# A hybrid decoder trunk: the mixer's 24 modulation tiles on GpSimd, ScalarE and VectorE instead of TensorE

## The chip, the cores and the metric

The kernel runs on one core of a Trainium2 chip. The core has a matrix engine (PE, TensorE), a vector engine (DVE, VectorE), a scalar engine (ACT, ScalarE), a general engine (POOL, GpSimd), and a queue (SP, SyncE) that issues most of the DMA transfers. Each engine works through its own instructions in order; semaphores order them against each other. PE writes its results into eight PSUM banks; everything else lies in SBUF. The metric is the device time of one execution in microseconds; a profiled execution gives, beside its time, a trace of every instruction.

## What is computed

Two layers over 256 positions of width 1024. Each layer has a mixer and a gated feed-forward, and each of these is wrapped in a modulation that a conditioning vector `c` sets:

```python
cs = jax.nn.silu(c)
mod = cs @ mod_w[layer] + mod_b[layer]          # 1024 -> 6 * 1024
sh1, sc1, g1, sh2, sc2, g2 = jnp.split(mod, 6, axis=-1)
h = rms_norm(x, norm_g[layer, 0]) * (1 + sc1) + sh1
x = x + g1 * mixer(h)       # layer 0: S5 state space + attention; layer 1: conformer convolution
h = rms_norm(x, norm_g[layer, 1]) * (1 + sc2) + sh2
x = x + g2 * conv_ffn(h)
```

The mixer of layer 0 projects `h` to a state-space part (32 groups of 16 channels with 64 complex states each) and to q, k, v of 8 heads. Their outputs are joined and projected. The change is about three of the twelve vectors of 1024: `g1`, `sc2` and `sh2` of layer 0, numbered 2, 4 and 3 in the code. They are matrix-vector products, each with a 1024 x 1024 block of `mod_w[0]`, that is 8 tiles of 128 x 1024 (512 KB each), 24 tiles in all. They are needed only after the mixer: the gate in `residual`, the scale and shift in `norm_gain` and `shift_cols`.

## The kernel before

All weights come as chunks of 128 x 1024 float32 in one order, `chunk_order`. `pump` issues the loads on SP in that order, each into the next free raw buffer: ten at the start (RAW_BUFS), four more, called ABT, when `s5_drive` has been placed. Most matmuls take float32 as a high and a low part: `split` has ACT copy a raw tile to `whi` and DVE subtract it to `wlo`, and three matmuls (high x high, high x low, low x high) make one product. `done` gives a raw buffer back and issues the next load.

The order of instructions on each engine is not the order of the text. `Plan` records every operation, estimates its cost and its dependences, and `arrange` places the operations of a stage by rank, which is the longest path behind an operation plus a hand-set or searched number per group (`BONUS`). The whole of `mixer0`, from the first load to the `glu` product, is one stage of this kind; the rest is placed in further stages. The matmuls of a bundle are placed as one.

The mixer stage computes, in this order of need: the layer's first modulation and the projection to u and q (`phase_a`); the poles, powers and tables of the state space (`s5_poles` to `s5_rot`, DVE and GpSimd, in the tile `arena` and the tile `CS`); k and v projections (`proj_k`, `proj_v`); the driven states (`s5_drive` on PE, `s5_state` on DVE: products with cosine and sine, four scans, and products again, the last of which writes Z); the outputs `s5_y` (PE, from KD, CA and Z); and attention by pairs of heads (`attn_score`, `attn_exp`, `attn_norm`, `attn_turn`, `attn_out`). Behind it `proj_o` multiplies the joined output with the abo chunks.

The three modulation vectors are made on PE between these. `mod_pe` takes each raw tile as the moving operand (512 columns at a time) and a 32-column version of `silu(c)`, `csv`, as the stationary one; four tiles go to four row groups of two banks, `B[6:8]`, which are the banks that `attn_turn` also uses. All 24 tiles add up in these two banks. Then `mod_evac` copies them to `mrow`, and `mod_sel` turns the rows into columns with eight small matmuls and adds the bias:

```python
nc.tensor.matmul(banks[half][g:g + 32, :], self.csv[:, j, f, :],
                 self.raw[("mp", l, s, f)][:, half * 512:half * 512 + 512], ...)
```

In the feed-forward of layer 0 other modulation tiles are already made on DVE, by `mod_dve`: one multiply of the raw tile by `cb` (silu(c) on every partition) with a running sum into one column of `modv`, and after eight of them the bias:

```python
self.nc.vector.scalar_tensor_tensor(self.junk, self.raw[c], 1.0, self.cb, op0=OP.mult, op1=OP.mult, accum_out=col)
```

Of the kernel before, what the change touches and what calls it, by code (L numbers as in the profile page):

```python
# [24 lines left out]
RAW_BUFS = 10  # L25
# [10 lines left out]
MD_STEP = (2, 1)  # L36
LN_MODS = [(1, 3), (1, 4)]
# [51 lines left out]
def chunk_order():  # L89
# [7 lines left out]
    def mp(l, s):  # L97
        return [("mp", l, s, f) for f in range(8)]

    a, b, c = mp(0, 2), mp(0, 4), mp(0, 3)  # L100
    order += [("k", 0), ("k", 1)] + a[:4] + [("k", 2), ("k", 3)] + a[4:]
    order += [("v", 0), ("v", 1)] + b[:4] + [("v", 2), ("v", 3)] + b[4:] + c
    order += [("abo", 4), ("abo", 5), ("glu", 0), ("glu", 1)]
    order += [("abo", i) for i in (6, 7, 0, 1, 2, 3)]
    md = [("md", l, s, f) for l, s in MD for f in range(8)]
    for i, c in enumerate(ffn_seq(0) + [("down", 0, i) for i in range(22)]):
        order.append(c)
        if md and i >= MD_FROM and (i % MD_STEP[0] < MD_STEP[1] if i < 44 else (i - 44) % MD_DOWN[0] < MD_DOWN[1]):
# [1972 lines left out]
```

## Time and profile before

| | us |
|---|---|
| median of 3 runs | 650.72 (647.98 to 651.05) |
| the profiled execution's time | 652.09 |
| its span, first to last instruction | 650.3 |

Nearly all instructions carry one line number, that of the planner's last line (L487), so they are told apart by the tiles that they write and read: `bank<-raw,csv` is a matmul of `mod_pe`, `wlo<-raw,whi` a low half, `junk<-raw,cb` a multiply of `mod_dve`. A matmul of float32 operands stands as two records. PEld is the weight load that goes with each matmul and overlaps it; its busy time is measured, while the end of a matmul is modelled. Times are from the span's start.

### The profile page before, as it was taken

The page shows a single profiled execution, that of the slowest core. Times are in us where ns is not written, and L with a number is a line of the kernel's source. Part 1 is how long each engine was busy: PE and PEld are TensorE (multiplying, and loading weights), DVE is VectorE, ACT ScalarE, POOL GpSimd, SP SyncE. Part 2 cuts the span into 40 slices and gives each one's busy share as a digit, 9 for nine tenths or more (in the row PEclk, how much of TensorE's full clock was granted, in tenths as well). Part 3 has the DMA queues.
Part 4 walks back from the last instruction along what each step waited for, and adds up shares of the span by engine and source line. Part 5 has one row for each costly group of instructions (what it writes and reads, how often), then busy time and mean ns, then how long its engine had stood idle before and what let it go on. Part 6 is the DMA issues. An engine that isn't in the chain of part 4 may idle for free.

```text
span 650.3 us, 13240 instructions
## 1 busy us (share of the span) xinstructions
PE 640.4 (98%) x5128; PEld 562.5 (87%) x5128; DVE 538.8 (83%) x1059; ACT 404.9 (62%) x736; POOL 41.2 (6%) x99
## 2 busy tenths in 40 slices
PE   8999999999999999999999999999999999999995
PEld 5789876899999999998899987568988888888885
DVE  8698996389999999999657999559999998997641
ACT  3479528897966666654446843377687766675431
POOL 4830000000000000000000222000000000000000
PEclk9999999999999999999999999999999999999998
DMA  8996888765489999999662798496476668764001
GB/s 325 405 377 224 291 324 300 316 217 210 134 288 320 325 331 303 338 328 365 195 196 81 245 325 245 154 380 263 135 280 199 201 214 259 217 210 164 1 0 66
DMA packets 45702, 158.50 MB, mean 244 GB/s; under 512 B 5535, under 2 KB 7112, under 8 KB 45640
## 3 DMA queue, kind: packets, MB, share of 16 engines
q1 hardware_dynamic: 43912, 153.84, 67.6%
q0 software_dynamic: 1152, 3.49, 1.9%
q8 instruction: 40, 0.66, 0.4%
q10 hardware_dynamic: 576, 0.33, 0.2%
q14 instruction: 22, 0.18, 0.1%
HBM read 153.10 MB, written 1.06 MB: 237 GB/s over the span
## 4 chain that ended last, share of the span: by engine, by line
PE 88%; DVE 7%; ACT 2%; DMA 1%; issue 1%; DVEq 0%; SPq 0%
PE bank L487 88%; DVE arena L487 4%; DVE wlo L487 1%; DMA raw<-w_in 1%; ACT CA L487 1%; DVE CS L487 1%; DVE U L487 1%; ACT whi L487 0%; ACT ABT L487 0%; DVE gp L487 0%; DVE nm L487 0%; DVE junk L487 0%; DVE h L487 0%; DVEq L2044 0%; DVE nt L487 0%
## 5 line engine op out<-in xcount | busy, mean ns | idle before, releaser
L487 PE MATMUL bank<-h,whi 128*128 128x256 f32 (+2 forms) x960 | 202.3, 303 | 0.2
L487 PEld LDWEIGHTS bank<-h,whi 128*128 128x128 f32 x960 | 152.4, 189 | 8.7 <-issue 1.0
L487 PE MATMUL bank<-h,wlo 128*128 128x256 f32 (+1 forms) x560 | 155.5, 283 | 0.0
L487 PE MATMUL bank<-h,whim 128*128 128x256 f32 (+1 forms) x664 | 149.1, 311 | 0.0
L487 PE MATMUL bank<-h,wlom 128*128 128x256 f32 x416 | 116.4, 281 | 0.0
L487 PEld LDWEIGHTS bank<-h,whim 128*128 128x128 f32 x664 | 108.2, 189 | 7.7
L487 PEld LDWEIGHTS bank<-h,wlo 128*128 128x128 f32 x560 | 104.5, 189 | 1.3 <-DVE CS L487 0.8
L487 DVE TENSOR_TENSOR wlo<-raw,whi 128x1024 fp32r<-128x1024 f32 x69 | 84.1, 1222 | 13.6 <-ACT whi L487 10.4
L487 ACT ACTIVATE whi<-raw 128x1024 fp32r<-128x1024 f32 x69 | 72.5, 1055 | 20.7 <-PE bank L487 13.7
L487 DVE TENSOR_TENSOR wlom<-raw,whim 128x1024 fp32r<-128x1024 f32 x60 | 72.9, 1222 | 10.5 <-ACT whim L487 10.3
L487 PEld LDWEIGHTS bank<-h,wlom 128*128 128x128 f32 x416 | 78.3, 188 | 0.1
L487 ACT ACTIVATE whim<-raw 128x1024 fp32r<-128x1024 f32 x60 | 62.6, 1054 | 22.7 <-PE bank L487 15.8
L487 PE MATMUL bank<-hv,whim 128*128 128x512 f32 (+1 forms) x236 | 67.7, 351 | 0.0
L487 PE MATMUL bank<-hv,whi 128*128 128x512 f32 x160 | 56.3, 393 | 0.0
L487 PE MATMUL bank<-hv,wlom 128*128 128x256 f32 x192 | 53.9, 281 | 0.0
L487 PEld LDWEIGHTS bank<-hv,whim 128*128 128x128 f32 x236 | 41.3, 189 | 6.2
L487 PE MATMUL bank<-hv,wlo 128*128 128x256 f32 x160 | 44.7, 279 | 0.0
L487 DVE SCALAR_TENSOR_TENSOR ac<-g,pp,ac 128x256 f32<-128x256 f32 x88 | 42.2, 482 | 2.5 <-ACT ac L487 0.8
L487 DVE SCALAR_TENSOR_TENSOR x<-bank,modv,x 128x256 f32<-128x256 f32 x54 | 25.6, 481 | 19.7 <-PE bank L487 19.1
L487 ACT ACTIVATE whi<-ABT 128x1024 fp32r<-128x1024 f32 x28 | 29.3, 1054 | 16.3 <-PE bank L487 15.3
L487 ACT ACTIVATE g<-bank 128x256 f32<-128x256 f32 x40 | 15.3, 382 | 36.4 <-PE bank L487 36.3
L487 PEld LDWEIGHTS bank<-hv,wlom 128*128 128x128 f32 x192 | 36.4, 190 | 0.0
(220 smaller groups left out, 1071.6 us busy)
## 6 DMA issues: line engine op xcount, KB each, us to landing
raw<-w_in SPq DMA_DIRECT2D x213, 512.0 KB, 5.3
ABT<-w_in SPq DMA_DIRECT2D x71, 512.0 KB, 4.9
a<-ap POOLq DMA_DIRECT2D x24, 142.0 KB, 5.4
x<-x_in SPq DMA_DIRECT2D x4, 256.0 KB, 4.2
arena<-scr SPq DMA_DIRECT2D x1, 1024.0 KB, 6.0
cb<-c_in SPq DMA_DIRECT2D x2, 512.0 KB, 4.9
kT<-bc_in SPq DMA_DIRECT2D x1, 512.0 KB, 11.4
out<-junk SPq DMA_DIRECT2D x2, 256.0 KB, 2.0
```

What stands on the lines that cost most here:

```text
L487: getattr(getattr(self.nc, eng), fn)(*a, **k)
```

## The change

The loads: the 24 chunks are packed the other way round, with 128 outputs on the partitions and the 1024 inputs along the row (`md` in place of `mp`), and they lie singly to threes between the chunks of k, v, abo and glu. The arithmetic: `mod_next` takes them one by one at written places of the mixer. Of three tiles, two are multiplied by `cb` on GpSimd in place and then copied by ACT with a running sum (`mod_pool`), and the third is one multiply with a running sum on DVE. `mod_bias` adds the bias to the columns at the end. `broadcast` makes `cb` for the mixer at the start: DVE multiplies the identity by silu(c), two matmuls with ones spread it over the partitions, ACT copies it out. `mod_pe`, `mod_evac` and `mod_sel` leave the mixer; `mod_pe` stays in the conformer. RAW_BUFS falls from 10 to 9, which makes room for the new tile. The planner's DMA rate goes from 370e3 to 390e3, and all numbers of BONUS are replaced, those of the loads too. ON_POOL leaves the later tiles on DVE, as they were.

```diff
-RAW_BUFS = 10
+RAW_BUFS = 9
...
+MIX_MOD = (1, 1, 0)
+ON_POOL = (0,)
...
-BONUS = {...}
+BONUS = {...}
...
-    a, b, c = mp(0, 2), mp(0, 4), mp(0, 3)
-    order += [("k", 0), ("k", 1)] + a[:4] + [("k", 2), ("k", 3)] + a[4:]
-    order += [("v", 0), ("v", 1)] + b[:4] + [("v", 2), ("v", 3)] + b[4:] + c
-    order += [("abo", 4), ("abo", 5), ("glu", 0), ("glu", 1)]
+    md = [("md", 0, s, f) for s in (2, 4, 3) for f in range(8)]
+    for c, n in zip([("k", 0), ("k", 1), ("k", 2), ("k", 3), ("v", 0), ("v", 1), ("v", 2), ("v", 3),
+                     ("abo", 4), ("abo", 5), ("glu", 0), ("glu", 1)], (1, 1, 1, 1, 2, 2, 2, 2, 3, 3, 3, 3)):
+        order += [c] + md[:n]
+        del md[:n]
...
-            return max(1.0 if op[4] == "rel" else 0.06, b / 370e3)
+            return max(1.0 if op[4] == "rel" else 0.06, b / 390e3)
...
+    def mod_pool(self, c):
+        _, l, s, f = c
+        w = self.raw[c]
+        self.nc.gpsimd.tensor_tensor(w, w, self.cb, op=OP.mult)
+        self.nc.scalar.activation(w, w, AF.Copy, accum_out=self.modv[l][:, s * 8 + f:s * 8 + f + 1])
+        self.done(c)
+
+    def mod_next(self, n):
+        for _ in range(n):
+            i = self.i_next
+            self.nc.group = "mod%d" % i
+            c = ("md", 0, (2, 4, 3)[i // 8], i % 8)
+            if MIX_MOD[i % len(MIX_MOD)]:
+                self.mod_pool(c)
+            else:
+                w = self.raw[c]
+                self.nc.vector.scalar_tensor_tensor(w, w, 1.0, self.cb, op0=OP.mult, op1=OP.mult,
+                                                    accum_out=self.modv[0][:, c[2] * 8 + c[3]:c[2] * 8 + c[3] + 1])
+                self.done(c)
+            self.i_next += 1
...
+    def broadcast(self):
+
+        nc = self.nc
+        cb = self.cb.rearrange("p (a b) -> p a b", b=128)
+        nc.vector.tensor_tensor(cb, self.ident.unsqueeze(1).to_broadcast([128, 8, 128]),
+                                self.cs.unsqueeze(2).to_broadcast([128, 8, 128]), op=OP.mult)
+        parts = (0, 4, self.aux[2]), (4, 8, self.aux[1])
+        for a, b, ps in parts:
+            nc.tensor.matmul(ps, self.ones, self.cb[:, a * 128:b * 128], start=True, stop=True)
+        for a, b, ps in parts:
+            nc.scalar.activation(self.cb[:, a * 128:b * 128], ps, AF.Copy, scale=float(D))
...
             self.split(("k", 2))
+            self.mod_next(2)
...
-            nc.group = "mod_pe004"
-            self.mod_pe(fg, 0, fb, 0, 4)
+            self.mod_next(1)
...
-            nc.group = "mod_pe048"
-            self.mod_pe(fg, 0, fb, 4, 8)
...
-            nc.group = "mod_pe1"
-            self.mod_pe(fg, 1, fb)
+            self.mod_next(2)
...
-            nc.group = "mod_pe2"
-            self.mod_pe(fg, 2, fb)
+            self.mod_next(1)
...
-            nc.group = "mod_evac"
-            self.mod_evac(fb)
+            self.mod_next(1)
...
-            nc.group = "mod_sel"
-            self.mod_sel(fg, B[0])
+            self.mod_next(1)
...
             self.attn_norm(2)
+            nc.group = "mod_bias"
+            for i in (2, 4, 3):
+                self.mod_bias(0, i)
```

The other calls of `mod_next(1)` and `mod_next(2)` stand between the remaining steps of the mixer, up to `attn_turn(1)`.

## Rows read from the trace of the kernel before

**Rows 1.** The page, part 1: busy time and share of each engine.

```profile
PE 640.4 (98%) x5128; PEld 562.5 (87%) x5128; DVE 538.8 (83%) x1059; ACT 404.9 (62%) x736; POOL 41.2 (6%) x99
```

**Rows 2.** Busy time by stretch: PE, PEld, DVE, ACT, POOL, then PEclk, DMA share, GB/s.

```profile
45.00:100.00 55.00, 54.91 (x455) 44.63 (x455) 51.42 (x102) 34.30 (x66) 1.10 (x1) 1.00 0.76 271
100.00:122.00 22.00, 22.00 (x388) 15.74 (x378) 10.38 (x30) 17.53 (x51) 0.00 (x0) 0.92 0.99 377
122.00:145.00 23.00, 23.00 (x193) 22.41 (x190) 14.98 (x25) 21.20 (x38) 0.13 (x2) 1.00 0.62 212
145.00:400.00 255.00, 255.00 (x2081) 243.79 (x2083) 232.76 (x406) 159.31 (x267) 11.48 (x23) 1.00 0.77 265
```

**Rows 3.** The chain of waits, in order of time: start, us, what.

```profile
80.52 7.55 DVE arena L487 x9
...
90.05 1.15 DVE wlo L487
...
91.24 88.83 PE bank L487 x914
...
419.94 7.17 DMA raw<-w_in
```

**Rows 4.** Timeline of PE, 100 to 113 us: start, us, engine line, operation.

```profile
100.69 1.06 PE L487 MATMUL bank<-arena,CA 128*32 128x63 f32 x64
...
103.93 0.60 PE L487 MATMUL bank<-ABT,csv 128*32 128x512 f32 x2
...
106.95 0.60 PE L487 MATMUL bank<-raw,csv 128*32 128x512 f32 x2
...
111.62 1.50 PE L487 MATMUL bank<-sel,mrow 128*128 128x3 f32 x12
```

**Rows 5.** PE's instruction groups, 40 to 130 us: records, busy us, mean ns.

```profile
L487 PE MATMUL bank<-raw,csv 128*32 128x512 f32 x80 | 11.3, 597 | 0.0
...
L487 PE MATMUL bank<-ABT,csv 128*32 128x512 f32 x16 | 3.9, 593 | 0.0
```

**Rows 6.** Timeline of DVE: the last two operations of `s5_state`.

```profile
98.82 1.28 DVE L487 TENSOR_TENSOR arena<-arena 128x512 f32<-128x512 f32 x2
```

**Rows 7.** `mod_dve` (ns min/median/max, first and last start) and ACT's high half.

```profile
L487 DVE SCALAR_TENSOR_TENSOR junk<-raw,cb x28: 1215/1218/1226, 161.1 to 582.9; 128x1024 f32<-128x1024 f32 x28
L487 DVE DVE_READ_ACCUMULATOR junk<-raw,cb x28: 80/83/88, 162.2 to 584.0; 128x1 f32 x28
...
L487 ACT ACTIVATE whi<-raw 128x1024 fp32r<-128x1024 f32 x9 | 9.4, 1054 | 1.3 <-DMA raw<-w_in 1.2
```

**Rows 8.** Timelines of POOL and DVE: its two wide copies, DVE meanwhile.

```profile
37.48 1.11 POOL L487 COPY D<-arena 128x1024 f32<-128x1024 f32 x1
...
37.80 0.81 DVE L487 SCALAR_TENSOR_TENSOR gp<-modv,gneg 128x1 f32<-128x1 f32 x1
...
42.96 0.16 DVE L487 SCALAR_TENSOR_TENSOR gp<-modv,gneg 128x1 f32<-128x1 f32 x1
...
73.85 1.10 POOL L487 COPY arena<-arena 128x1024 f32<-128x1024 f32 x1 [35.08 <-DMA arena<-scr]
...
73.97 1.88 DVE L487 TENSOR_TENSOR arena<-bank,CS 128x512 f32<-128x512 f32 x3
```

**Rows 9.** DVE's groups from 45 to 100 us with a PSUM input, and reductions.

```profile
L487 DVE TENSOR_TENSOR arena<-bank,CS 128x512 f32<-128x512 f32 x6 | 3.8, 682 | 0.0
...
L487 DVE SCALAR_TENSOR_TENSOR CS<-bank,arena 128x384 f32<-128x384 f32 x4 | 2.1, 555 | 0.3 <-DVE U L487 0.2
L487 DVE TENSOR_REDUCE U<-CS 128x1 f32<-128x256 f32 x4 | 1.5, 411 | 0.0
...
L487 DVE TENSOR_TENSOR U<-bank,CS 128x512 f32<-128x512 f32 x2 | 1.4, 683 | 0.0
...
L487 DVE TENSOR_REDUCE U<-CS 128x1 f32<-128x128 f32 x4 | 0.9, 275 | 0.0
```

**Rows 10.** One stretch of 1 us, columns as in rows 2.

```profile
114.00:115.00 1.00, 1.00 (x6) 0.74 (x3) 1.00 (x4) 1.00 (x4) 0.00 (x0) 0.50 1.02 418
```

More of the change, by code (lines that the diff above doesn't have):

```diff
@@ L98, in mp @@
         return [("mp", l, s, f) for f in range(8)]
-    a, b, c = mp(0, 2), mp(0, 4), mp(0, 3)
-    order += [("k", 0), ("k", 1)] + a[:4] + [("k", 2), ("k", 3)] + a[4:]
-    order += [("v", 0), ("v", 1)] + b[:4] + [("v", 2), ("v", 3)] + b[4:] + c
-    order += [("abo", 4), ("abo", 5), ("glu", 0), ("glu", 1)]
+    md = [("md", 0, s, f) for s in (2, 4, 3) for f in range(8)]
[3 more added lines that the diff above has]
+        del md[:n]
+    assert not md
     order += [("abo", i) for i in (6, 7, 0, 1, 2, 3)]
@@ L564, in __init__ @@
         self.raw = {}
+        self.i_mod = 0
+        self.i_next = 0
         self.slots = {}
@@ L646, in feed, with mod, mod_bias @@
                     break
-                (self.mod_dve if c[0] == "md" else self.split)(c)
+                (self.mod if c[0] == "md" else self.split)(c)
             self.pos += 1
         self.auto = True
+    def mod(self, c):
+        self.i_mod += 1
+        (self.mod_pool if ON_POOL[self.i_mod % len(ON_POOL)] else self.mod_dve)(c)
+        if c[3] == 7:
+            self.mod_bias(*c[1:3])
+    def mod_pool(self, c):
[17 more added lines that the diff above has]
+            self.i_next += 1
+    def mod_bias(self, l, s):
+        mc = self.modcols(l, s)
+        self.nc.vector.tensor_tensor(mc, mc, self.par("modb", l * 48 + s * 8, 8), op=OP.add)
     def mod_dve(self, c):
@@ L656, in mod_dve @@
         self.done(c)
-        if f == 7:
-            mc = self.modcols(l, s)
-            self.nc.vector.tensor_tensor(mc, mc, self.par("modb", l * 48 + s * 8, 8), op=OP.add)
     def low(self, n):
@@ L1784, in start @@
             nc.tensor.matmul(self.mm[i % 4][:, 0:n], self.zero[:, 0:128], self.zero[:, 0:n], start=(i < 4), stop=False)
+        nc.group = "bcast"
+        self.broadcast()
         nc.group = "poles"
@@ L1834, in mixer0 @@
             self.arena = t([128, ARENA], F32, name="arena")
+            self.cb = t([128, 1024], F32, name="cbm")
             self.cut = 0
@@ L1912, in mixer0 @@
             vb = B[4:6]
+            self.mod_next(1)
             nc.group = "proj_v0"
@@ L1916, in mixer0 @@
             self.split(("v", 2))
+            self.mod_next(1)
             nc.group = "proj_v1"
@@ L1920, in mixer0 @@
             self.split(("v", 3))
-            nc.group = "mod_pe1"
-            self.mod_pe(fg, 1, fb)
+            self.mod_next(2)
             nc.group = "proj_v2"
             self.proj_v(2, vb)
+            self.mod_next(1)
             nc.group = "score0"
             self.attn_score(0, B[0:2])
+            self.mod_next(2)
             nc.group = "proj_v3"
@@ L1931, in mixer0 @@
                 nc.scalar.activation(self.v[:, t_, :], vb[t_], AF.Copy)
-            nc.group = "mod_pe2"
-            self.mod_pe(fg, 2, fb)
+            self.mod_next(1)
             nc.group = "exp0"
             self.attn_exp(0, B[0:2])
+            self.mod_next(1)
             nc.group = "norm0"
@@ L1939, in mixer0 @@
             self.attn_score(1, B[2:4])
-            nc.group = "mod_evac"
-            self.mod_evac(fb)
+            self.mod_next(1)
             nc.group = "exp1"
             self.attn_exp(1, B[2:4])
+            self.mod_next(1)
             nc.group = "y0"
             self.s5_y(0, B[4])
-            nc.group = "mod_sel"
-            self.mod_sel(fg, B[0])
+            self.mod_next(1)
             nc.group = "norm1"
@@ L1951, in mixer0 @@
             self.attn_turn(0, (B[6], B[7]))
+            self.mod_next(1)
             nc.group = "y1"
             self.s5_y(1, B[5])
+            self.mod_next(1)
             nc.group = "out0"
             self.attn_out(0, B[1])
+            self.mod_next(1)
             nc.group = "score2"
             self.attn_score(2, B[2:4])
+            self.mod_next(1)
             nc.group = "exp2"
             self.attn_exp(2, B[2:4])
+            self.mod_next(1)
             nc.group = "turn1"
             self.attn_turn(1, (B[6], B[7]))
+            self.mod_next(1)
             nc.group = "y2"
```

2 lines of the change are left out of this document (1 added, 1 removed).

## The prediction

> **What bounds the kernel now.** I read the page first, then the stretches of the mixer, then the chain of waits, and only then single instructions. The page puts PE at 98% of the span [rows 1], which invites the reading that every matmul taken off PE is time won. The stretches correct that. From 122 us on the weight loads, which are not modelled, fill 22.4 of 23 us and then 243.8 of 255: PE really is the bound there. From 45 to 100 us they fill 44.6 of 55, while DVE works 51.4 of the same 55 [rows 2]. The chain of waits says the same: it runs through DVE (the last long pieces are the state's arena operations and a low half, wlo) until 91.2 us, and from there through PE in one piece of 88.8 us [rows 3]. So the mixer has two parts. Before about 91 us the vector engine sets the pace, and the state Z, which `s5_y` needs, is finished by DVE only at 98.82 + 1.28 = 100.1 us [rows 6]. After that PE sets it. The change works in both parts, and not with the same sign.
>
> **What it removes.** The 48 matmuls of `mod_pe` are 96 records [rows 5]; `mod_sel` follows. What of them lies on the chain? Those before 100.69 us fill PE while DVE still works on Z: the first matmul with CA starts 0.6 us after Z is done [rows 4, 6]. Without them PE would wait there, so I count nothing for them; if DVE had been early, the 3.5 us from 97.2 to 100.7 would count as well. Those from 103.93 to 107.55 us are on the path: 3.6 us [rows 4]. `mod_sel` takes 1.4 us for twelve of its sixteen records (111.62 to 113.05) [rows 4], and the other four at that pace 0.4, so 1.8. Removed from the path: **-5.4 us**, at most -8.9.
>
> **What it adds on DVE.** A third of the 24 tiles, eight, are one multiply with a running sum: 1.22 us and 0.08 for reading the sum out, from the same operation in the feed-forward, 1.30 us each [rows 7]. Which come before Z? In the order of the loads md0 to md9 stand ahead of the last v tile, whose low half was the piece at 90 us [rows 3], so those ten are in SBUF by then. Of them 2, 5 and 8 go to DVE: 3 x 1.30 = **+3.9 us**. The other five fall after 100 us, where DVE works 10.4 of 22 us [rows 2]: nothing, and 6.5 us if that room is gone. `broadcast` (one 128x1024 multiply on DVE, two matmuls, two evictions) falls at the start, where the a0 loads pace the work; I take nothing, and 1.2 us for its DVE operation by the nearest row of that width if it is not covered [rows 7].
>
> **What it adds on ScalarE.** Sixteen sums of 128x1024, each near the 1.05 us of a high half plus a read-out [rows 7], some 18 us, against two evictions saved. ACT works 34.3 of 55 us and 17.5 of 22 [rows 2]: 25 us are free in the two stretches. I take nothing. If the cover is missing at one spot, the price is a raw buffer held one sum longer, about 1 us for the load behind it.
>
> **What it adds on GpSimd, and whom that stops.** Seven of the ten early tiles (0, 1, 3, 4, 6, 7, 9) are multiplied on GpSimd, which is nearly empty. Its time for this operation is not in the trace. The nearest row is a copy of the same width, with one input: 1.10 us [rows 8]. That is the lower end; two inputs taken one after the other give 2.2, which I use as the nearest to a multiply. The Trainium skill's page "GPSIMD Engine Reference", section 3.1, puts a two-input operation at about 2.6 cycles an element at 1.2 GHz, an estimate of 2.2 us for 1024; no run here shows it, and the sum by it would be the one below.
>
> GpSimd's own time would be hidden. What matters is what DVE does meanwhile. During the copy at 37.48 us (1.11 us, so until 38.59) DVE had a 128x1 operation with two SBUF inputs (modv, gneg). It started at 37.80 and took 0.81 us instead of the 0.16 of the same operation at 42.96: it ended with the copy. During the second copy at 73.85 us three DVE operations with one input in PSUM went through in 1.88 us, undisturbed [rows 8]. So on this chip a DVE operation that reads two SBUF tensors stands still while GpSimd reads. That the whole of a two-input multiply holds DVE off, no row shows. The Trainium skill's page "SBUF — State Buffer", section "Who interferes with whom", says it does: the two engines share a port pair, the one that starts first has it for its whole instruction, and DVE with one SBUF input is exempt. The trace agrees for the copy (0.81 against 0.16 us); by that rule the sum is mine, and if the multiply let DVE in half-way it would be half of the lock term.
>
> The DVE work at stake is mostly of the kind that is stopped. From 45 to 100 us the groups with a PSUM input or a reduction come to 3.8 + 2.1 + 1.4 + 1.5 + 0.9 = 9.7 us [rows 9], and DVE is idle 55 - 51.4 = 3.6 us [rows 2]. A multiply falls on such time with a share of 13.3 / 55 = 24%. So the lock costs the state's chain 7 x 2.2 x 0.76 = **+11.7 us**. Below: nothing, if GpSimd happens to run only in the stretch of PSUM operations around 74 to 78 us. Above: ten multiplies and no overlap, 22 us. Behind the stopped DVE operation stand, in its queue, the low halves of the v tiles (PE waits for them), then Z (PE waits in `s5_y`), then the softmax's first additions. The later nine multiplies fall on a DVE that is half idle: nothing.
>
> **Buffers and loads.** RAW_BUFS goes from 10 to 9. At 419.9 us the chain runs 7.2 us through a load [rows 3]; one tile less fetched ahead there is one tile's transfer more, 512 KB at 377 GB/s [rows 2]: **+1.4 us** (0 if that load was late for another reason). The 24 tiles are the same bytes as before. SP issues loads in order, each when its buffer is free, and now a buffer is freed by GpSimd and then ACT. The abo and glu tiles stand behind md tiles; the abo loads are wanted from 122 us on. The planner's new bonuses reorder every queue; no row prices that, and I take nothing and let the range hold it.
>
> **Sum.** -5.4 + 3.9 + 11.7 + 1.4 = +11.6 us. The profiled execution took 652.1 us (650.3 of span and 1.8 around it), so 663.7; it lies 1.4 above the median of the runs, 650.7, which gives **662 us** for a median.
>
> **Rivals.** *The lock is hidden, PE's saving stays (faster).* The place is Z's end. If DVE's order puts its PSUM operations and its idle time under the multiplies, and the state's chain first, Z moves by less than 5.4 us, which is the point from which it decides; GpSimd may also be held off by DVE's back-to-back work instead of the reverse. For it: GpSimd has 77 us for its work (45 to 122), and mod_pe and mod_evac no longer sit in front of `attn_turn` at 108 us. Against it: DVE has 3.6 us of idle time in 55. Time: 650.7 - 5.4 to - 8.9, so 642 to 645. Chance 0.33.
>
> *A wash.* The lock bites at its lower price: 7 x 1.1 x 0.76 = 5.9, and the DVE tiles slip behind Z: -5.4 + 5.9 + 1.4 = +1.9, 652.6. It includes the case that the two parts cancel. Chance 0.12.
>
> *The delay spreads (slower still).* GpSimd falls behind, md buffers stay full, SP cannot issue abo, and PE starves at 122 us as well. The top of the lock term, 22 + 3.9 + 1.4 - 5.4 = +21.9, gives 672.6. A starved PE can also lose its clock: around 114 us, in a stretch in which weight loads fill 15.7 of 22 us [rows 2], the granted clock was 0.50 [rows 10], its lower level, 1.2 GHz, for some 3 us; one more dip is 1.6 us of PE work. Chance 0.12.
>
> **How the numbers follow.** My forecast, slower by 4 to 15 us, has 0.43; its own range is 655 to 666. Differences under 0.5% (3.3 us) cannot be told from no change. Slower is 0.43 + 0.12 = 0.55, same 0.12, faster 0.33. Cases of both signs hold much of the chance, so the range runs from the full saving, 642, to the full lock, 672; outside it I leave a little on either side for the new order of the queues.
>
> **What would show it.** In the changed kernel's profile: DVE operations of 1.22 us and 0.68 us stretched to 2 or 3 us between 45 and 105 us, ending with a GpSimd multiply; multiplies of about 2.2 us, longer where they wait for DVE; the last arena operation before the first CA matmul at 113 to 118 us instead of 100; weight loads thinner before that; from `proj_o` on PE full as before. The prediction is wrong if DVE's means in that stretch stay at 1.22 and 0.68 us, if Z is done by 105 us, or if `proj_o` starts before 122 us.

## The result

| | before | after |
|---|---|---|
| median of the runs, us | 650.84 (647.98 to 651.05) | 677.53 (674.67 to 679.73) |
| ratio after to before | | 1.0418 (95%: 1.0369 to 1.0468) |
| profiled execution, span, us | 650.3 | 678.0 |

The kernel became 26.7 us slower. The forecast was 11.3 us slower (662, range 642 to 672): the direction held, the size did not, and the time lies outside the range.

All of the loss is made ahead of the residual of layer 0. That operation first runs at 147.4 us before and at 176.5 us after; from there to the last residual it is 493.8 us before and 492.4 after. So the profile after has to be read between 45 and 147 us. The page's first part and the busy time by stretch, columns as in [rows 1, 2]:

```profile
PE 641.3 (95%) x5020; PEld 569.5 (84%) x5020; DVE 575.4 (85%) x1076; ACT 421.0 (62%) x768; POOL 88.3 (13%) x115
```

```profile
45.00:100.00 55.00, 43.58 (x400) 40.98 (x399) 52.44 (x80) 40.60 (x76) 23.66 (x10) 0.89 0.71 263
100.00:122.00 22.00, 8.14 (x32) 6.22 (x33) 22.00 (x18) 4.42 (x6) 14.29 (x5) 0.66 0.27 100
122.00:145.00 23.00, 22.71 (x230) 16.94 (x230) 22.01 (x51) 20.06 (x57) 6.13 (x1) 0.93 0.86 288
145.00:400.00 255.00, 254.35 (x2088) 245.52 (x2087) 225.01 (x386) 171.97 (x301) 5.27 (x9) 1.00 0.74 259
```

From 100 to 122 us PE works 8.1 of 22 us, where it worked all of them [rows 2], and DVE is busy for the whole 22 with only 18 instructions, 1.2 us each. The chain of waits after shows whose they are; its long piece is six operations of the state that take 15.35 us:

```profile
96.80 2.97 DVE arena L491 x4
...
100.37 15.35 DVE arena L491 x6
...
119.85 1.22 DVE wlo L491
```

GpSimd's multiplies in 45 to 122 us, grouped, and the timelines of POOL and of DVE beside them:

```profile
L491 POOL TENSOR_TENSOR raw<-raw,cbm 128x1024 f32<-128x1024 f32 x11 | 29.1, 2661 | 32.0 <-DMA raw<-w_in 25.5 <-PE bank L491 6.5
L491 POOL TENSOR_TENSOR ABT<-ABT,cbm 128x1024 f32<-128x1024 f32 x3 | 7.9, 2625 | 1.6 <-DMA ABT<-w_in 1.5
```

```profile
55.64 2.37 POOL L491 TENSOR_TENSOR raw<-raw,cbm 128x1024 f32<-128x1024 f32 x1 [3.01 <-DMA raw<-w_in]
...
100.78 5.19 POOL L491 TENSOR_TENSOR ABT<-ABT,cbm 128x1024 f32<-128x1024 f32 x2 [1.49 <-DMA ABT<-w_in]
105.94 6.49 POOL L491 TENSOR_TENSOR raw<-raw,cbm 128x1024 f32<-128x1024 f32 x2
112.39 2.78 POOL L491 TENSOR_TENSOR ABT<-ABT,cbm 128x1024 f32<-128x1024 f32 x1
129.97 6.13 POOL L491 TENSOR_TENSOR raw<-raw,cbm 128x1024 f32<-128x1024 f32 x1 [14.81 <-DMA raw<-w_in]
```

```profile
77.33 3.29 DVE L491 TENSOR_TENSOR wlo<-raw,whi 128x1024 fp32r<-128x1024 f32 x1
80.55 1.22 DVE L491 SCALAR_TENSOR_TENSOR raw<-raw,cbm 128x1024 f32<-128x1024 f32 x1
...
103.65 6.63 DVE L491 TENSOR_TENSOR_SCAN arena<-D,arena 128x512 f32<-128x512 f32 x2
110.21 5.51 DVE L491 TENSOR_TENSOR arena<-arena,CS 128x512 f32<-128x512 f32 x2
```

Fourteen multiplies start before 115 us and take 37.0 us. An undisturbed one takes 2.37 us. The scans show the lock at work: two of them take 6.63 us from 103.65, and the two multiplies beside them 6.49 us from 105.94. Each engine's instruction waits for the whole of the other's. The cost by kind of operation, DVE's groups from 45 to 122 us after:

```profile
L491 DVE TENSOR_TENSOR wlo<-raw,whi 128x1024 fp32r<-128x1024 f32 x9 | 13.0, 1449 | 0.7 <-ACT whi L491 0.7
L491 DVE TENSOR_TENSOR_SCAN arena<-D,arena 128x512 f32<-128x512 f32 x4 | 11.1, 2821 | 0.0
L491 DVE TENSOR_TENSOR arena<-arena,CS 128x512 f32<-128x512 f32 x6 | 8.0, 1383 | 0.0
L491 DVE TENSOR_TENSOR arena<-arena,U 128x512 f32<-128x512 f32 x3 | 4.6, 1519 | 0.0
L491 DVE TENSOR_TENSOR arena<-bank,CS 128x512 f32<-128x512 f32 x6 | 3.8, 677 | 0.1
```

The same groups before, from 45 to 102 us (`arena<-bank,CS` is in [rows 9]):

```profile
L487 DVE TENSOR_TENSOR wlo<-raw,whi 128x1024 fp32r<-128x1024 f32 x8 | 9.7, 1220 | 0.0
L487 DVE TENSOR_TENSOR_SCAN arena<-D,arena 128x512 f32<-128x512 f32 x4 | 4.6, 1206 | 0.0
...
L487 DVE TENSOR_TENSOR arena<-arena,CS 128x512 f32<-128x512 f32 x6 | 3.8, 680 | 0.0
L487 DVE TENSOR_TENSOR arena<-arena,U 128x512 f32<-128x512 f32 x4 | 2.7, 684 | 0.0
```

A scan goes from 1206 to 2821 ns, a product of two SBUF tiles from 680 to 1383, the product with a PSUM operand from 682 to 677: stopped and exempt operations stand side by side in one trace. These four groups alone lose 9 x 0.23 + 4 x 1.62 + 6 x 0.70 + 3 x 0.84 = 15.3 us. What PE sees of it, PE's timeline after:

```profile
121.12 0.80 PE L491 MATMUL bank<-wlo,h 128*128 128x512 f32 x1 [13.43 <-DVE wlo L491]
...
138.73 1.09 PE L491 MATMUL bank<-arena,CA 128*32 128x63 f32 x64
```

PE stood 13.4 us for the low half of a v tile, which stood behind the stretched operations in DVE's queue. The first CA matmul came at 138.7 us instead of 100.7 [rows 4]. The last write of Z, on DVE's timeline after, ends at 128.73 + 0.68 = 129.4 us instead of 100.1 [rows 6]:

```profile
128.73 0.68 DVE L491 TENSOR_TENSOR arena<-arena 128x512 f32<-128x512 f32 x1
```

Z is 29.3 us late and the residual 29.1, so what delays Z is what the kernel loses.

### The profile page after: what moved, and what is told of

It reads as the page before. It is cut to its first block, busy times and chain, and to the rows that moved or that the text cites. A ratio compares the mean times of both kernels' runs of the same rounds, so it can differ in the third digit from the quotient of the medians.

```text
span 678.0 us, 13113 instructions
## 1 busy us (share of the span) xinstructions
PE 641.3 (95%) x5020; PEld 569.5 (84%) x5020; DVE 575.4 (85%) x1076; ACT 421.0 (62%) x768; POOL 88.3 (13%) x115
## 4 chain that ended last, share of the span: by engine, by line
PE 81%; DVE 9%; POOL 3%; ACT 2%; issue 2%; DMA 2%; DVEq 0%; SPq 0%
PE bank L491 81%; DVE arena L491 6%; POOL arena L491 3%; DVE wlo L491 1%; DMA raw<-w_in 1%; ACT CS L491 1%; DMA pp<-pp_in 0%; ACT whi L491 0%; ACT arena L491 0%; DVE U L491 0%; DMA ABT<-w_in 0%; DVE gp L491 0%; DVE CS L491 0%; DVE h L491 0%; DVE nm L491 0%
## 5 line engine op out<-in xcount | busy, mean ns | idle before, releaser
L491 PEld LDWEIGHTS bank<-h,whi 128*128 128x128 f32 x960 | 154.0, 193 | 8.9 <-DVE h L491 0.8
L491 PE MATMUL bank<-h,wlom 128*128 128x256 f32 x416 | 116.2, 281 | 0.0
L491 DVE TENSOR_TENSOR wlo<-raw,whi 128x1024 fp32r<-128x1024 f32 x74 | 92.0, 1247 | 8.5 <-ACT whi L491 8.3
L491 ACT ACTIVATE whi<-raw 128x1024 fp32r<-128x1024 f32 x74 | 77.5, 1055 | 29.6 <-PE bank L491 21.9
L491 DVE TENSOR_TENSOR wlom<-raw,whim 128x1024 fp32r<-128x1024 f32 x53 | 64.7, 1220 | 11.8 <-ACT whim L491 11.6
L491 ACT ACTIVATE whim<-raw 128x1024 fp32r<-128x1024 f32 x53 | 55.8, 1054 | 29.3 <-PE bank L491 17.7
L491 POOL TENSOR_TENSOR raw<-raw,cbm 128x1024 f32<-128x1024 f32 x13 | 37.6, 2909 | 66.6 <-DMA raw<-w_in 60.1
L491 ACT ACTIVATE whim<-ABT 128x1024 fp32r<-128x1024 f32 x28 | 29.5, 1056 | 20.8 <-PE bank L491 12.3
L491 DVE SCALAR_TENSOR_TENSOR x<-bank,modv,x 128x256 f32<-128x256 f32 x54 | 25.5, 481 | 19.2 <-PE bank L491 18.5
L491 DVE TENSOR_TENSOR wlom<-ABT,whim 128x1024 fp32r<-128x1024 f32 x28 | 34.1, 1220 | 4.6 <-ACT whim L491 4.4
```

The costliest lines, as they stand in the source:

```text
L491: getattr(getattr(self.nc, eng), fn)(*a, **k)
```

## The experiments

Each row of the table is the median less the median of the kernel before run on the same chip (649.1 to 650.3). Six of them (e1, e8, e12, e13, e16, e17) leave vectors out, as their expectations say.

| run | what | us over before |
|---|---|---|
| e1 | after, multiplies on GpSimd replaced by memsets | +8.2 |
| e12 | e1 and DVE's multiplies cut to 8 columns | +5.8 |
| e16, e17 | after, only the first nine, only the last seven multiplies | +16.7, +13.5 |
| e2 | after, all 24 tiles on DVE | +26.4 |
| e3, e7 | before with nine buffers: with 16 GpSimd squares, without | +29.8, +15.1 |
| e10, e11 | the same without and with squares, order written out | +10.3, +25.0 |
| e18 | before, ten buffers, squares, every queue as it was | +22.2 |
| e8 | before, PE's modulation matmuls narrowed | -1.1 |
| e9 | before, nine buffers, third vector on DVE, as planned | +25.3 |
| e14, e15 | before, ten buffers, third vector on DVE; on GpSimd | +11.8, +15.6 |
| e4, e5 | after with some, with all bonuses of before | +49.2, +45.1 |
| e6 | before with the bonuses of after | +25.2 |
| e13 | e12 with ten buffers | +45.2 |

**The lock.** e1 keeps every queue of the kernel after and gives GpSimd the same time without reading:

```diff
-gpsimd.tensor_tensor(w, w, cb, op=OP.mult)
+for n in (1024, 1024, 512):
+    gpsimd.memset(w[:, 0:n], 1.0)
```

> The changed kernel in which each of the 16 multiplies on GpSimd is replaced by three memsets of the same tile (1024, 1024 and 512 elements, so about as long), with every engine's order kept; the modulation vectors are then not those of the reference. A memset reads nothing from SBUF. Theory (lock: a DVE operation with two SBUF inputs stands still while GpSimd reads): the scans of the state return from 3.4 to 1.2 us, Z is ready some 20 us earlier, and the time falls to 652 to 662 us. Rival (the new order of loads and queues, or the buffers held by GpSimd and ScalarE): the same buffers are held as long as before, so 672 to 678 us.

Measured: 658.0 (656.6 to 659.0), ratio 1.0125 (1.0108 to 1.0142). The scans take 1.2 us again, as this row of DVE's timeline of e1 shows, though GpSimd works 34 us of the 55 between 45 and 100:

```profile
85.87 1.20 DVE L495 TENSOR_TENSOR_SCAN arena<-D,arena 128x512 f32<-128x512 f32 x1
```

So the multiplies' reading cost 26.7 - 8.2 = 18.5 us, and GpSimd's being busy without reading cost the scans nothing. The Trainium skill's page "SBUF — State Buffer", section "Who interferes with whom", has both halves: a two-input DVE instruction contends with a GpSimd instruction that reads SBUF, not with one that only writes it. The trace agrees (2821 against 1199 to 1218 ns for a scan).

In e1 the last write of Z ends at 106.8 us instead of 129.4. Fourteen of its sixteen groups of memsets begin ahead of that, as fourteen multiplies did ahead of Z in the kernel after, so it is not the lock that brought so many ahead of Z. What the lock's delay moves is what they fall beside: ahead of the end of the last scan begin nine in e1 (87.1 us) and thirteen in the kernel after (110.3 us).

e3 put 16 unused squares of raw tiles (1.9 us each) into the kernel before:

```diff
-RAW_BUFS = 10
+RAW_BUFS = 9
+gpsimd.tensor_tensor(spare, raw, raw, op=OP.mult)   # 16 of the 24 tiles of mod_pe
```

> The kernel before, with RAW_BUFS 9, and with 16 multiplies of 128x1024 on GpSimd added whose results nobody reads (each squares a raw tile of mod_pe into a spare tile; a raw buffer is then free when both PE and GpSimd have read it). PE's modulation, the bonuses and the loads are those of before. Lock theory: the lock alone slows it, 663 to 676 us, with DVE operations of two SBUF inputs stretched. Rival (order, loads): 650 to 654 us.

Measured: 679.6 (675.8 to 683.3), ratio 1.0458 (1.0413 to 1.0504). I first read this as a lock of 30 us; e7 showed that half of it was the buffer and the order that came with it.

> The kernel before with nine raw buffers. By the term of the prediction's sum: 1.4 us more, 651 to 652. By the stretch behind the residual, which was as long in every run so far with nine as with ten: no change, 649.5 to 650.5. A rival: the mixer itself lives on the tenth buffer, 655 or more, with the v tiles later.

Measured: 665.2 (662.9 to 666.8), ratio 1.0233 (1.0194 to 1.0271): the rival, not my term. Since the planner places the whole mixer anew for any edit that it sees, e10 and e11 wrote out the order that it had given with ten buffers:

```diff
+REF = "..."                                   # the order of before, operation by operation
+order = like_before(ops, pred)                # as in REF, as far as the dependences let it
```

> The kernel before with nine raw buffers as in e7, but the mixer's operations are placed in the very order that the planner gave with ten (a written list; only what a buffer forces moves). It splits the 15 us of e7. If the order that the planner found for nine is what costs: 649.5 to 652. If the tenth buffer itself is what the mixer lives on: 662 to 667 as in e7. In between: both.

> e10 with the 16 unused squares of e3 on GpSimd, each placed just ahead of the PE matmuls that read the same tile, all other queues in the old order: the price of the lock with nothing else moved. By the prediction's term (each GpSimd operation of 1.9 us that begins before Z costs 1.9 x 0.76 = 1.4 us; 7 to 10 of them): 10 to 14 us above e10. By the difference of e3 and e7: 14.4 above e10. If the new order in e3 was part of its loss: 8 or less above e10.

Measured: 660.6 (659.8 to 662.7), ratio 1.0156 (1.0127 to 1.0185), and 675.4 (673.6 to 676.9), ratio 1.0377 (1.0346 to 1.0407). The difference, 14.7 us, equals that of e3 and e7. The scans of e11 take 1.2 us each; eight squares fall between them and Z, which ends at 123.0 us instead of 106.7. The squares also hold their raw tiles longer, and that share was not measured by itself. ACT's and DVE's timelines of e10 show the buffer's part:

```profile
86.10 1.06 ACT L494 ACTIVATE whi<-raw 128x1024 fp32r<-128x1024 f32 x1 [6.43 <-DMA raw<-w_in]
```

```profile
87.19 1.22 DVE L494 TENSOR_TENSOR wlo<-raw,whi 128x1024 fp32r<-128x1024 f32 x1 [5.33 <-ACT whi L494]
...
88.93 4.56 DVE L494 TENSOR_TENSOR_SCAN arena<-D,arena 128x512 f32<-128x512 f32 x4
```

Up to 81 us the state's operations come on DVE as early as in the kernel before. Then a v tile lands late, its low half stands in DVE's queue ahead of the scans, and they start at 88.9 us instead of 82.3.

> The kernel before with ten buffers and every queue in its own old order; 16 unused squares of raw tiles (1.9 us each) run on GpSimd into mrow, each placed just ahead of PE's matmuls of the same tile. The lock and the held tiles alone. By e11 against e10: 14.7 us, 664 to 666. If a part of that was the missing buffer: 656 to 660. By the prediction's rule for the 7 to 10 ahead of Z, 1.9 x 0.76 each: 660 to 664.

Measured: 671.2 (667.3 to 673.5), ratio 1.0325 (1.0295 to 1.0355), more than any theory. The squares write `mrow`, so `mod_evac` comes late too (130.5 us instead of 107.4), but that is not where the time goes: Z already ends at 120.9 us instead of 100.1, and up to 116 us the chain of waits of e18 stays on DVE, whose operations are stretched. So the squares cost some 20 us here, with the order and the buffers of before. Why more than in e11 was not tried.

e16 and e17 split the multiplies at the table copy:

```diff
+if self.count > 9:      # e16; e17: <= 9
+    memsets as in e1
```

> The kernel after; the nine multiplies that GpSimd does ahead of the copy of the relative-position table stay, the seven behind it are memsets as in e1 (those vectors are not computed). With the prediction's rule (2.2 x 0.76 = 1.7 us for each one ahead of Z, nothing for the others): 658 + 9 x 1.7 = 673. If each of the sixteen costs the same 19.5 / 16 = 1.2 us: 669. If the late ones are the costly ones, since they hold the scans and the softmax: 662 to 665.

> The kernel after; the nine multiplies ahead of the table copy are memsets, the seven behind it stay. By the prediction's rule (those behind Z cost nothing; some of the seven are ahead of it): 658 to 664. At 1.2 us each: 666.5. If the late ones are the costly ones: 671 to 675.

Measured: 665.7 (665.4 to 666.5), ratio 1.0246 (1.0215 to 1.0276), and 662.6 (660.4 to 666.6), ratio 1.0206 (1.017 to 1.0242). Above e1 that is 8.5 us for nine and 5.3 for seven; together in the kernel after they cost 18.5. Neither group is free, and the two together cost more than their sum. The traces show where: Z ends at 116.2 us with the nine alone, at 106.7 with the seven alone, as early as with none (106.8), and at 129.4 with all. Alone, the late ones run beside operations behind the scans, where DVE waits for ACT in e1; in the kernel after, where the nine have already delayed DVE, four of them run beside the last two scans and the products behind them.

**DVE's tiles and what is left.**

> The kernel after in its own order, the 16 GpSimd multiplies replaced by memsets as in e1, and the 8 DVE multiplies cut to 8 columns (the three vectors are not computed). If the 8 us that were left in e1 are the new order: 655 to 658, nothing gained over e1. If they are DVE's tiles: 648 to 652. With PE's own 5.4 us won on top, as the prediction has it, and nothing else: 645.

Measured: 656.2 (652.0 to 661.0), ratio 1.0092 (1.0067 to 1.0117). DVE's tiles are worth about 2 us, though the two intervals overlap. With no tile multiplied at all the kernel is still 5.8 us slower than before. The chain of waits of e12 names a wait that I had counted at nothing:

```profile
79.24 9.45 DMA arena<-scr
...
88.84 2.36 POOL arena L497
...
99.13 0.96 POOL ABT L493
100.14 0.54 POOL ABT L493
...
100.70 1.15 ACT ABT L497 x2
...
101.88 1.28 ACT L497
...
103.58 1.45 ACT CS L497 x7
```

The softmax's exponentials (`CS` on ACT) stand in ACT's queue behind the sums of tiles, the sums wait for GpSimd, and GpSimd's queue holds the relative-position table's copy ahead of those tiles, itself late for its DMA. The chain of e1 runs the same way. Its DVE timeline has the wait, and Z stands behind it in DVE's queue:

```profile
103.88 0.18 DVE L495 RECIPROCAL U<-U 128x4 f32<-128x4 f32 x1 [3.75 <-ACT CS L495]
```

Up to the scans e1 loses nothing: DVE writes the first part of `h` at 22.2 us instead of 15.1, yet the last scan starts at 85.9 as against 85.7. Between there and the last write of Z it loses 6.7 us, and the residual is 6.7 late (154.1 instead of 147.4). That the wait for ACT accounts for all of this was not tried by itself.

```diff
-RAW_BUFS = 9
+RAW_BUFS = 10     # e12 with the order of after written out
```

> e12 (the kernel after in its own order, no tile multiplied) with ten raw buffers, the order of the queues written out as in e12 (the broadcast is left out, since nothing reads it; the vectors are not computed). If the 6 us left in e12 are the tenth buffer: 647 to 651. If they are the new order: 655 to 657, no change from e12. The 10.3 us of e10 need not appear in full, since the new order of loads was searched for nine.

Measured: 695.3 (692.8 to 696.4), ratio 1.0692 (1.0668 to 1.0716). It tells nothing of the question: its chain waits for raw tiles (8.3, 3.3, 6.0 and 5.1 us between 135 and 163). I take it that an order written for nine buffers hands the ten to other loads; that was not followed up. How the 5.8 us divide between ACT's queue, the buffer and the order stays open.

```diff
-MIX_MOD = (1, 1, 0)
+MIX_MOD = (0,)
```

> The changed kernel with all 24 tiles multiplied and summed on DVE (MIX_MOD = (0,)), nothing on GpSimd. Lock theory: 16 multiplies that stop DVE for up to 2.4 us each give way to 16 operations of 1.3 us, so although DVE now does 21 us more work of its own the time falls, to 660 to 670 us. Rival (DVE is overloaded by its own work and GpSimd was relief): 685 to 698 us.

Measured: 676.2 (675.5 to 676.8), ratio 1.0406 (1.039 to 1.0421). It lies between the two theories. No scan is stretched, but sixteen tiles of 1.2 us stand ahead of the scans on DVE, which start at 100.2 us instead of 82.3, and the chain waits there for the loads of two such tiles (5.1 and 6.8 us). The planner placed the mixer anew here, so the tiles and the order are not separated: as slow as the lock, by another road.

**PE's saving.** e8 narrows the matmuls that the change removes and moves nothing else:

```diff
-matmul(banks[half][g:g + 32, :], csv, raw[..., 512 columns])
+matmul(banks[half][g:g + 32, 0:16], csv, raw[..., 16 columns])    # 40 of 48
```

> The kernel before, each engine in its old order; of mod_pe's matmuls the 40 that only add to the sum read 16 columns in place of 512 (the vectors are thus not those of the reference; loads, waits and buffers stay). It prices what PE gets back. By the prediction only the stretch of 103.9 to 107.6 us is on the path: 3 to 3.6 us less, 646 to 647. If PE is the limit all through the mixer, 80 records of 0.6 us less their rest: 10 us or so less, 640. If PE waits for DVE or the loads anyway, or its clock falls in the gaps: 649 to 652.

Measured: 649.0 (646.5 to 652.6), ratio 0.9987 (0.9966 to 1.0008). That is 1.1 us of the 3.6 that the prediction had put on these matmuls, and not clear of no change. PE, which waited for nothing between 90 and 145 us before, waits 4.3 us there in e8, 1.9 of them for Z. `mod_sel`, for which the prediction had another 1.8, was left as it is.

**A part of the change by itself.** e9 and e14 take only the third vector off PE:

> The kernel before, with the third vector alone on DVE: its eight tiles loaded the other way round, each multiplied with a running sum on DVE at the place in the order where PE's matmuls of it stood (planned behind Z), nothing on GpSimd, nine buffers, the broadcast at the start. By the prediction's terms: PE 3 us less, DVE's 8 x 1.3 = 10.4 us in the 11.6 us of 100 to 122 in which it was idle: 646 to 648, and faster than both kernels. Rival: the softmax's additions stand behind the tiles on DVE and PE waits for them: 652 to 656. Rival: the planned place falls ahead of Z on the chip: up to 10 us more, 655 to 660, with the first CA matmul late.

> The kernel before with its own order and ten buffers; the third vector alone is taken off PE: its eight tiles are multiplied with a running sum on DVE, four of them right behind Z and four at the place where PE's matmuls stood; silu(c) for all partitions comes by a DMA on GpSimd's queue and one ScalarE operation (with a table load) into the unused mrow, while ScalarE is idle. By e8, which took 1.1 us off with nearly all of PE's modulation gone: 648 to 650, no change that can be told. By the prediction's 3.6 us on the path: 646 to 647. Rival: DVE's 10.4 us behind Z hold up the softmax: 653 or more.

> e14 with six of the eight tiles multiplied on GpSimd and summed on ScalarE, the other two on DVE, all behind Z. It prices the lock there. By the prediction, which counted the multiplies behind Z at nothing: within 1 us of e14. Rival: six times 2.4 us on a DVE that PE waits for in the softmax, or ScalarE held at the sums while GpSimd works: 4 to 12 us above e14.

Measured: 675.4 (674.5 to 680.0), ratio 1.0403 (1.0361 to 1.0445); 661.8 (659.8 to 662.2), ratio 1.0172 (1.0153 to 1.0192); 665.7 (663.7 to 672.5), ratio 1.0253 (1.0219 to 1.0288). In e9 the buffer, the broadcast and the new order come with the tiles and were not separated; Z ends at 113.2 us, against 107.0 in e7, before the first tile runs. e14 keeps the order and the ten buffers; beside the tiles it has a load of c and a silu for the multiplier. Its DVE and PE timelines:

```profile
100.12 1.22 DVE L499 SCALAR_TENSOR_TENSOR raw<-raw,mrow 128x1024 f32<-128x1024 f32 x1
...
104.70 0.61 DVE L504 SCALAR_TENSOR_TENSOR KD<-ident,pp,KD 128x128 f32<-128x128 f32 x2
```

```profile
105.19 2.09 PE L504 MATMUL bank<-u,KD 128*128 128x256 f32 x8 [4.21 <-DVE KD L504]
...
114.58 0.90 PE L504 MATMUL bank<-anti,CS 128*128 128x128 f32 x3 [3.92 <-ACT mrow L504]
```

Four tiles behind Z take the 4.6 us before KD is written, and PE waits 4.2 for KD. The second wait, 3.9 us, is partly the experiment's: silu(c) lies in `mrow`, which `mod_evac` may write only when the tiles are done. Around these waits PE's granted clock falls, as the stretches of e14 show in the seventh number, PEclk: 0.83, 0.61 and 0.68, where the kernel before had 1.00, 0.86 and 1.00 with PE busy throughout (means of a stretch; 0.50 is the lower of the two levels, 1.2 GHz):

```profile
100.00:110.00 10.00, 5.79 (x149) 4.62 (x141) 7.70 (x16) 4.52 (x14) 0.00 (x0) 0.83 0.57 211
110.00:122.00 12.00, 8.08 (x36) 5.97 (x32) 8.49 (x17) 7.27 (x18) 0.00 (x0) 0.61 0.93 358
122.00:134.00 12.00, 12.00 (x181) 9.84 (x182) 3.55 (x14) 6.41 (x20) 0.00 (x0) 0.68 0.75 301
```

Moving six of the eight tiles to GpSimd, with their sums on ScalarE, costs 3.8 us more (e15).

**The order.** e4, e5 and e6 exchange the bonuses:

```diff
-BONUS = {...}      # of the one kernel
+BONUS = {...}      # of the other: e4 the first loads', e5 and e6 all
```

> The changed kernel with the bonuses of the first loads (x, c, identity, the a0 and uq chunks, bc) set back to those of the kernel before, all else as changed. Start theory: the first normalised feature came 6.9 us later in the changed kernel (20.5 against 13.6 us) and the last one 7.3 us, so 668 to 672 us. Lock alone: DVE is behind anyway, the loads at the start do not matter, 675 to 679 us.

> The kernel after with all bonuses of the kernel before (the new groups have none). If the order of the queues matters little beside the lock: 673 to 680. If the new bonuses are what makes the change bearable, as e6 and e7 suggest that any order other than the one searched for costs 15 to 25 us: 690 to 705. If the new bonuses are themselves the loss: 660 or less.

> The kernel before with the bonuses of the kernel after for every group that both have (mod_pe, mod_evac and mod_sel keep theirs): PE still makes the three vectors, only the order of the queues is the new one. If the loss of the change is the lock and the tiles alone: 649 to 653. If the new order costs something by itself (the first feature began 7 us later in the kernel after): 655 to 660, with the first feature at 18 to 21 us. If the new order is as bad as a half of the loss: 663 or more.

Measured: 699.0 (697.0 to 700.0), ratio 1.0747 (1.0725 to 1.0769); 695.5 (694.3 to 696.4), ratio 1.0685 (1.0654 to 1.0716); 675.2 (673.6 to 677.7), ratio 1.0389 (1.0354 to 1.0424). My idea behind e4, that the new order of the first loads cost the start, fell: with the old one the first feature came no earlier (24.3 against 24.0 us) and the kernel lost another 22 us. Each set of bonuses fits its own kernel alone: the other's costs 25 us in the kernel before (e6) and 18 in the kernel after (e5).

No version here that computes the vectors beats the kernel before. e8 says why no further one was built: with 40 of the 48 modulation matmuls cut to almost nothing there are 1.1 us to win in this order. Another search of the order was not tried.

## Why the prediction was right in direction and wrong in size

Term by term the forecast of 11.3 us and the 26.7 measured differ so: 6.8 us more for the lock (18.5 against 11.7), 1.5 less for DVE's tiles (2.4 against 3.9), and 9.8 more for all the rest, which the prediction had at -5.4 + 1.4 = -4.0 and which measured +5.8 (e12). So two steps failed: the count of the multiplies that the lock acts through, and the rest, where PE's saving was taken as sure while ScalarE's sums and the new order stood at nothing. (That makes 15.1 of the 15.4 us; 0.3 went in rounding the forecast to 662.)

- **GpSimd's lock, +11.7.** Right in mechanism: DVE's operations on two SBUF tiles stood still for whole multiplies, those with a PSUM operand did not, and the multiply took 2.37 us for the assumed 2.2 (the Trainium skill's page "GPSIMD Engine Reference", section 3.1, whose 2.6 cycles an element had given the same estimate of 2.2, was 7% low here). The step that failed is the count: "Seven of the ten early tiles" and, for the rest, "The later nine multiplies fall on a DVE that is half idle: nothing". Fourteen started before 115 us, ahead of Z, and took 37.0 us. I had counted the tiles that are loaded ahead of the last v tile; but Z comes later than that tile, and GpSimd takes each tile as it lands, so that fourteen are ahead of Z even with the lock gone (e1). The later ones were not free either (e17: 5.3 us, e15: 3.8), and behind a DVE that the first nine have delayed they cost more. Measured: 18.5 in the kernel after; 14.7 and 22.2 for squares in the old order (e11, e18). The rate was too high: 2.2 x 0.76 = 1.7 us each, against 0.9 for the nine early ones alone and 18.5 / 14 = 1.3 if all of the loss is put on those ahead of Z. With the right count it would have given 23.4 us, so the low count and the high rate partly made up for each other, and that is luck. The prediction's words that DVE with one SBUF input is exempt are too wide as well; see the last section.
- **Matmuls off PE, -5.4.** Of this, 3.6 stood for the matmuls of `mod_pe`: measured 1.1 (e8). The 1.8 for `mod_sel` was not tried. A stretch in which PE is busy is not on the path for that alone: as PE's work went, waits for DVE and ACT came in its place (4.3 us in e8).
- **Tiles on DVE, +3.9.** About 2 (2.4, e12 against e1). One tile ran ahead of Z, at 80.55 us, not three. That those behind Z are free, because DVE is idle there, was wrong as a rule: in e14 four of them cost PE 4.2 us of waiting, since what PE needs next stood behind them.
- **ScalarE's sums, nothing.** Wrong: I asked whether ACT had time, not what stands behind a sum that waits for GpSimd. It was the softmax, and behind it Z: DVE waits 3.75 us for it in e1. It is part of the 5.8 us; how large a part stays open, and so does the price of the new order.
- **Ten to nine buffers, +1.4.** Wrong place. At 420 us nothing was lost, 493.8 against 492.4 us. In the mixer of before the tenth buffer was worth 10.3 us (e10). What it is worth in the new order is open.
- **The rivals.** Of "the delay spreads" the bound was 672.6 by ten multiplies without overlap; its outcome came true: from 100 to 122 us the loads fell to 100 GB/s from 377, PE starved, and its mean granted clock was 0.66. GpSimd did not fall behind, though: it waited 14.8 us for its next tile at 130 us. PE was held by the low half on DVE. "The lock is hidden" and "a wash" fell.
- **What would show it.** Stretched operations, the multiplies' length and a full PE from `proj_o` on came as written. The last arena operation before the first CA matmul was to end at 113 to 118 us and ended at 129.4.

By measurement, taking one thing away after the other, the 26.7 us are: 18.5 for the multiplies' reading (e1), 2.4 for DVE's tiles (e12), and 5.8 for the rest, in which whatever the change wins on PE is already counted. In another order of taking away, the shares could differ.

## What to carry to other kernels

A lock between two engines is not priced by what is loaded ahead of one early point: count all of the locking work that can start before the locked chain ends, and ask beside which of its operations each piece falls, since every delay moves the later pieces (nine multiplies cost 8.5 us, seven 5.3, all sixteen 18.5). Ask for each idle stretch what stands behind the added work in the queue. Before work is taken off a busy engine, narrow it in place and see what comes back; here that was 1.1 us where 3.6 were hoped for. And where the order of the queues was searched for, an edit that makes the planner place it anew, or takes a buffer, can cost more than the work that it moves.

## What the runs showed of the hardware

GpSimd is held as DVE is. In e1 the copy of 128x1024 that took 1.10 us before [rows 8] took 6.42 us while DVE ran operations on two SBUF tiles without a pause, and ended when they paused; POOL's and DVE's timelines of e1:

```profile
88.08 6.42 POOL L495 COPY arena<-arena 128x1024 f32<-128x1024 f32 x1 [2.45 <-DMA arena<-scr]
```

```profile
89.37 2.49 DVE L495 TENSOR_TENSOR arena<-arena,CS 128x512 f32<-128x512 f32 x4
91.78 0.68 DVE L495 TENSOR_TENSOR arena<-arena,U 128x512 f32<-128x512 f32 x1
92.39 1.22 DVE L495 TENSOR_TENSOR wlo<-raw,whi 128x1024 fp32r<-128x1024 f32 x1
94.53 1.02 DVE L495 SCALAR_TENSOR_TENSOR CS<-bank,arena 128x384 f32<-128x384 f32 x2 [0.93 <-POOL arena L495]
```

A copy with one SBUF input can be held too. Of the four copies of `u` in the kernel after, three take 0.28 us as before; the fourth, at 74.92 us, takes 2.38 and ends with the multiply that began at 74.45. DVE's groups after and before:

```profile
L491 DVE COPY U<-u 32x256 f32<-32x256 f32 x4 | 3.2, 806 | 0.1
```

```profile
L487 DVE COPY U<-u 32x256 f32<-32x256 f32 x4 | 1.1, 283 | 0.1
```

So one SBUF input alone does not exempt a DVE operation. The section of the Trainium skill's page "SBUF — State Buffer" that the prediction cites says it of instructions "outside the 2-port perf modes"; the prediction left this condition out. Whether this copy runs in such a mode, no run here shows.

A memset of 128x1024 on GpSimd (0.95 us) held none of e1's scans. A square, which reads one tile twice, took 1.9 us where the product of two tiles took 2.37.
